# Recurrence layer: casts of summed weights and copies out of PSUM laid out as waiting tasks

## The chip, the cores and the metric

The kernel runs as one program on one core of a Trainium2 chip. The metric is the device time of one execution in microseconds (us). The engines of the core are TensorE (PE: matmuls, with weight loads PEld beside them), VectorE (DVE), ScalarE (ACT), GpSimd (POOL) and SyncE (SP), which here issues most DMA transfers. Each engine runs its instructions in the order of the program and waits on semaphores for the others.

## The reference

A decoder trunk of two layers on one sequence of 1024 rows and 1024 columns. The first layer mixes tokens with a gated linear recurrence of 8 heads of 128 columns, the second with attention in a window; each is followed by a gated feed-forward part with a convolution. Only the first mixer is touched:

```python
q, f, i, g = jnp.split(h @ w_in, 4, axis=-1)
fg = lb + (1.0 - lb) * jax.nn.sigmoid(heads(f))
o = hgrn2_chunkwise(jax.nn.silu(heads(q)), 1.0 - fg, heads(i), jnp.log(fg))
o = o * lax.rsqrt(jnp.mean(jnp.square(o), -1, keepdims=True) + RMS_EPS)
o = o * g_norm_w * jax.nn.silu(heads(g))
return o.reshape(B, S, D) @ w_out
# hgrn2_chunkwise: S_t = diag(f_t) S_{t-1} + k_t v_t^T ; o_t = S_t^T q_t
```

All values are float32.

## The kernel before, in words

The recurrence layer fills the span from about 45 to 535 us. Matmuls of float32 operands are made of three passes (lines 194, 195, 196): high part by high part, high by low, low by high. A high part is a cast on ACT, the low part is a subtraction on DVE (line 169).

**Units and products.** Head 0 is projected directly. The other heads come as units, two per head: `q` (columns of q and f) and `v` (columns of i and g), numbered 0 to 13. A unit is a product of 2x2 blocks made with seven block products instead of eight, p = 1 to 7, which need sums of blocks of the weights and of the input. Each product has 12 matmuls of 128x512 in one of four PSUM banks (`psmm`, buffers 489 to 492). The units run in the order p = 1, 5, 4 (of the unit before), 6, 2, 3, 7.

**Weights.** `unit_load` loads a unit's raw weights by SP into a pair of buffers (raw0 and raw1 for `q`, raw2 and raw3 for `v`; raw_99 to raw_102 in the order's rows). `prepare` makes the weights of the next unit's products while a unit runs: `cast` puts the high part into the tile `WR` on ACT (L1243), and a job makes the low part on DVE (L169). The products 5, 6, 7 and 4 need a sum of blocks first, made in place on DVE (L1250, and L1449 for unit 0).

**Recurrence of a head.** `recur(h)` runs for head h between the products: DVE builds up products of decay over levels (qp, kp and tot, L1089 to L1094), PE makes the scores (`psax` from L200), DVE picks them by masks into `Ab` (L1032, L1053), ACT copies them into `A`, PE transposes kp and the values VT (L204) and multiplies. `turn_values` transposes VT for the next head's use and applies the gate of g. `norm` scales by the mean square, with a power on POOL, and transposes og.

**Out of PSUM.** `collect` takes each product out of its bank: ACT copies the first (L1298 for p=1, L1308 for p=6, L1310 for p=5 or 7, L1349 for VT's second half), DVE adds the second to it (L1342, L1315, L1322).

**What sets the order.** The code is run once on the host with a model of time in the class `Order`: `od.t` is the modelled time of PE, `od.v` that of DVE. A task is a generator that yields the time it waits; `tick`, called between matmuls, steps the tasks whose time has come and lays waiting DVE jobs (`lay_job`) while DVE's modelled queue is short. `need` lays jobs until a certain one is out. `drive` steps all tasks until a condition holds. What comes out is a fixed order of instructions for each engine; the times in the model are not measured.

Of the kernel before, what the change touches and what calls it, by code (L numbers as in the profile page):

```python
# [16 lines left out]
P = 128  # L17
# [90 lines left out]
def trunk(ctx: ExitStack, tc: tile.TileContext, a: dict, out: bass.AP):  # L108
# [591 lines left out]
    with tc.tile_pool(name="t", bufs=1, reuse_waits="tile") as raws, hgrn_pool as hp:  # L700
# [529 lines left out]
        units = [(kind, h) for h in range(1, NH) for kind in "qv"]  # L1230
        raw_of, guard, ready, gated, turned = {}, [[] for _ in range(4)], [], {0}, set()
# [5 lines left out]
        def unit_load(u):  # L1237
            kind, h = units[u]
            raw_of[u] = [halves(column(g, h)) for g in ((0, 1) if kind == "q" else (2, 3))]
# [6 lines left out]
        def prepare(u, stage):  # L1246
            if u >= len(units):
                return
            (b11, b21), (b12, b22) = [(r[:, 0], r[:, 1]) for r in raw_of[u]]
# [10 lines left out]
            else:  # L1260
                after, src = {5: (1, b11), 6: (2, b22), 7: (3, b12), 4: (4, b21)}[stage]
                need(("sum", u, after))
                cast(u, stage, src)

        def product(u, p):
            need(("lo", u, p))
            ps, w = bank(u, p), WR[0][:, row_of(u, p), :]
            od.finish(guard[banks.index(ps)])
            guard[banks.index(ps)] = []
# [10 lines left out]
        state, sigs, turning = {}, [], []  # L1280
# [4 lines left out]

        def collect(u, p, ps):
            kind, h = units[u]
            n = banks.index(ps)
            if p == 1:
                state[u] = {"n": 0}  # L1290
                if kind == "q":
                    if u:
                        drive(lambda: gates_read[0] >= h - 1)
                    state[u]["q"] = hp.tile([P, S], F32, name="qs" if u else "og")
                else:
                    drive(lambda: all(t[1] is None for t in sigs) and queries_done[0] >= 0)
                    sigs.clear()
                nc.scalar.copy((state[u]["q"] if kind == "q" else VT)[:, :512], ps)  # L1298
                return
            st = state[u]  # L1300
            if p in (5, 6, 7) and "c" not in st:
                if kind == "q":
                    drive(lambda: (queries_done if h > 1 else gates_read)[0] >= h - 1)
                else:
                    drive(lambda: h < 2 or h - 2 in turned)
                st["c"] = hp.tile([P, S], F32, name="fg") if kind == "q" else flat(gates[h % 2])
            if p == 6:
                nc.scalar.copy(st["c"][:, :512], ps)  # L1308
            elif p in (5, 7) and "half" not in st:
# [656 lines left out]
```

## Time and profile before

| what | us |
|---|---|
| median of 3 runs | 2181.5 (2179.52 to 2184.3) |
| the profiled execution, its own time | 2183.3 |
| its span in the profile | 2181.5 |
| PE busy in the span | 2112.6 |

The granted clock of PE in the profiled execution was 0.983 on the mean. A line of a view names the engine, the line of the kernel's file, the operation, what it writes and reads (out<-in), and the shape. In brackets stands how long the engine was idle before it and what ended the idle time. psmm and psax are PSUM banks; T and HL hold the input's parts and sums, WR the weights' parts.

### The profile page before, as it was taken

What the parts mean: (1) busy time and instruction counts of PE and PEld (TensorE: products, weight loads), DVE (VectorE), ACT (ScalarE), POOL (GpSimd) and SP (SyncE); (2) the same over time, 40 slices, a digit from 0 to 9 for tenths busy, and PEclk for the clock granted to TensorE, in tenths of its full rate; (3) what the DMA queues carried; (4) which work ended last, traced back from release to release, by engine and by line L of the source; (5) the groups of instructions that cost most, each with busy time, mean ns of one, the idle gap of its engine ahead of it and who ended that gap; (6) DMA issues with size and microseconds to landing.
All of it is one profiled execution on the core that took longest, in us unless ns stands there. A gap on an engine that the chain in (4) does not pass through costs nothing.

```text
span 2181.5 us, 31770 instructions
## 1 busy us (share of the span) xinstructions
PE 2112.6 (97%) x12303; PEld 1758.8 (81%) x12303; DVE 1800.1 (83%) x2459; ACT 973.5 (45%) x1570; POOL 254.2 (12%) x278
## 2 busy tenths in 40 slices
PE   9789999998899999999999999999999999999998
PEld 7667777787688888888888888888888888888887
DVE  6677777765899999997897858978999999978986
ACT  6454445562344444444443256752454444444430
POOL 1000000000103112110000203231021122100001
PEclk9899999999999999999999999999999999999999
DMA  4011111132324547754965431133245577549662
GB/s 158 20 39 42 49 49 49 51 100 95 118 97 153 176 154 168 164 131 147 325 226 183 159 79 34 45 100 114 91 136 179 164 160 167 137 136 321 233 207 102
DMA packets 241488, 286.82 MB, mean 131 GB/s; under 512 B 30089, under 2 KB 160313, under 8 KB 241337
## 3 DMA queue, kind: packets, MB, share of 16 engines
q1 hardware_dynamic: 222464, 238.26, 33.6%
q0 software_dynamic: 18016, 46.16, 10.2%
q8 instruction: 97, 1.59, 0.3%
q14 instruction: 55, 0.44, 0.1%
q10 hardware_dynamic: 856, 0.37, 0.1%
HBM read 241.72 MB, written 89.15 MB: 152 GB/s over the span
## 4 chain that ended last, share of the span: by engine, by line
PE 92%; DVE 5%; ACT 1%; DMA 1%; issue 0%; SPq 0%; DVEq 0%; ACTq 0%
PE psmm L194 18%; PE psmm L196 18%; PE psmm L195 18%; PE psax L194 9%; PE psax L195 9%; PE psax L196 9%; PE psax L200 4%; PE psmm L204 1%; PE psmm L200 1%; PE psax L204 1%; PE psax L1740 1%; DVE WR L169 1%; DVE qp L1089 1%; DVE Ab L1032 1%; PE psmm L1574 1%; DVE kp L1091 1%
## 5 line engine op out<-in xcount | busy, mean ns | idle before, releaser
L498 DVE SCALAR_TENSOR_TENSOR Y<-Y,cwt 128x1023 f32<-128x1023 f32 (+1 forms) x176 | 224.9, 1281 | 48.8 <-ACT Y L496 47.5
L221 ACT CAST HL<-rx 128x1024 fp32r<-128x1024 f32 (+1 forms) x151 | 150.8, 1006 | 147.6 <-DMA rx<-in_ffn_w_in_dram 28.8
L194 PE MATMUL psmm<-T,HL 128*128 128x512 f32 x512 | 200.7, 392 | 0.0
L196 PE MATMUL psmm<-T,HL 128*128 128x512 f32 x512 | 199.4, 389 | 0.0
L195 PE MATMUL psmm<-T,HL 128*128 128x512 f32 x512 | 199.3, 389 | 0.0
L169 DVE TENSOR_TENSOR HL<-rx,HL 128x1024 fp32r<-128x1024 f32 (+1 forms) x151 | 178.4, 1187 | 15.0 <-ACT HL L221 14.8
L496 ACT ACTIVATE Y<-Y,cwt 128x1024 f32<-128x1024 f32 x88 | 108.7, 1238 | 91.5 <-DVE Y L485 86.3
L194 PE MATMUL psax<-T,HL 128*128 128x512 f32 x352 | 137.3, 390 | 0.0
L196 PE MATMUL psax<-T,HL 128*128 128x512 f32 x352 | 137.0, 389 | 0.0
L195 PE MATMUL psax<-T,HL 128*128 128x512 f32 x352 | 137.0, 389 | 0.0
L243 POOL TENSOR_TENSOR rs<-rs,nhalf 128x1 f32<-128x1 f32 x32 | 44.4, 1388 | 738.1 <-DVE rs L242 738.1
L196 PEld LDWEIGHTS psmm<-T,HL 128*128 128x128 f32 x512 | 96.1, 188 | 20.2
L194 PEld LDWEIGHTS psmm<-T,HL 128*128 128x128 f32 x512 | 96.2, 188 | 19.6
L195 PEld LDWEIGHTS psmm<-T,HL 128*128 128x128 f32 x512 | 96.2, 188 | 19.4
L540 POOL COPY warm<-Y 128x1 f32<-128x1 f32 x64 | 64.6, 1009 | 355.4 <-DVE Y L479 350.7
L221 ACT CAST HT<-rx 128x1024 fp32r<-128x1024 f32 (+1 forms) x37 | 35.5, 959 | 133.8 <-DVE rx L452 59.0
L196 PE MATMUL psmm<-T,WR 128*128 128x512 f32 x224 | 89.7, 401 | 5.6 <-DVE WR L169 5.6
L194 PE MATMUL psmm<-T,WR 128*128 128x512 f32 x224 | 91.5, 409 | 2.7 <-ACT WR L1243 2.7
L169 DVE TENSOR_TENSOR WR<-raw,WR 128x512 fp32r<-128x512 f32 x98 | 63.8, 686 | 30.6 <-ACT WR L1243 30.6
L195 PE MATMUL psmm<-T,WR 128*128 128x512 f32 x224 | 88.7, 396 | 0.0
L221 ACT CAST HL<-Y 128x1024 fp32r<-128x1024 f32 (+1 forms) x32 | 28.6, 892 | 117.8 <-DVE Y L452 41.5
L1243 ACT CAST WR<-raw 128x512 fp32r<-128x512 f32 x98 | 58.5, 621 | 48.3 <-DVE raw L1250 30.6
(414 smaller groups left out, 6011.9 us busy)
## 6 DMA issues: line engine op xcount, KB each, us to landing
rx<-in_ffn_w_in_dram SPq DMA_DIRECT2D x136, 256.0 KB, 4.1
rx<-gd SPq DMA_DIRECT2D x118, 256.0 KB, 3.4
bsd<-in_ffn_w_out_dram POOLq DMA_DIRECT2D x36, 768.0 KB, 7.3
gd<-Y SPq DMA_DIRECT2D x44, 512.0 KB, 2.9
raw<-in_hgrn_w_in_dram SPq DMA_DIRECT2D x30, 512.0 KB, 4.1
rx<-in_ffn_w_out_dram SPq DMA_DIRECT2D x54, 256.0 KB, 4.7
R<-bsd SPq DMA_DIRECT2D x44, 256.0 KB, 5.0
Y<-in_ffn_w_in_dram SPq DMA_DIRECT2D x40, 256.0 KB, 4.0
```

Source lines behind the costliest of these rows:

```text
L169: make = lambda e: e.tensor_tensor(lo, src, hi.bitcast(F32), op=ALU.subtract)
L194: nc.tensor.matmul(ps, st(0), mv(0), start=start, stop=False, skip_group_check=more)
L195: nc.tensor.matmul(ps, st(0), mv(1), start=False, stop=False, skip_group_check=more)
L196: nc.tensor.matmul(ps, st(1), mv(0), start=False, stop=stop, skip_group_check=more)
L200: nc.tensor.matmul(ps, lhsT, rhs, start=start, stop=stop, **kw)
L204: nc.tensor.transpose(ps, src, ident)
L221: nc.scalar.copy(hi, src)
L243: nc.gpsimd.tensor_tensor(rs, rs, nhalf, op=ALU.pow)
L496: nc.scalar.activation(c, u, AF.Identity, bias=cwt[:, l, 3, ci:ci + 1], scale=cwt[:, l, 2, ci:ci + 1])
L498: nc.vector.scalar_tensor_tensor(c[:, sh:], u[:, :S - sh], cwt[:, l, 2 - sh, ci:ci + 1], c[:, sh:], op0=ALU.mult, op1=ALU.add)
L540: with tc.issue_after(nc.gpsimd.tensor_copy(tick, Y[:, 2 * (fc % 2) + (p == 4), :1]).ins):
L1243: nc.scalar.copy(w[:, :512], src)
```

## The change

The work is the same on every engine, instruction for instruction; only its order changes. Four things are done.

- The casts of summed weights (products 5, 6, 7, 4) become tasks, `cast_sum`, that wait until the sum has been laid out and until DVE's modelled time has been reached by PE's. A product drives the tasks until its cast is out.
- The copies out of PSUM become tasks (`keep_first`, `keep`, `add_to`, `sum11`), which are laid out when their own conditions hold, instead of driving all others until they do. `clear` waits for a bank's tasks. `drive` now steps the earliest task and moves the modelled time on.
- The raw loads of a later unit and of the output weights become tasks that wait for the low part of p=4.
- The sums of the input are made in another order (those for p=5 ahead of those for p=3), and `first_unit` no longer has all sums of unit 0's weights laid out ahead of the first head's recurrence.

The diff, cut to its core:

```diff
...
             return ROW[p] if p in ROW else (6 if u % 2 else 7)
 
         def unit_load(u):
+            while u > 1 and ("lo", u - 2, 4) not in done_jobs:
+                yield 0.2
             kind, h = units[u]
             raw_of[u] = [halves(column(g, h)) for g in ((0, 1) if kind == "q" else (2, 3))]
 
...
         def prepare(u, stage):
             if u >= len(units):
                 return
+            drive(lambda: u in raw_of)
             (b11, b21), (b12, b22) = [(r[:, 0], r[:, 1]) for r in raw_of[u]]
             plus = lambda key, x, y: job(0.0, 0.61, lambda: tt(x, x, y, op=add), ("sum", u, key))
             if stage == 0:
...
                 cast(u, 2, b21)
                 plus(4, b21, b22)
             else:
-                after, src = {5: (1, b11), 6: (2, b22), 7: (3, b12), 4: (4, b21)}[stage]
-                need(("sum", u, after))
-                cast(u, stage, src)
+                prep[u, stage] = od.spawn(cast_sum(u, stage, *{5: (1, b11), 6: (2, b22), 7: (3, b12), 4: (4, b21)}[stage]))
+
+        def cast_sum(u, p, after, src):
+            while ("sum", u, after) not in done_jobs:
+                yield 0.2
+            yield max(od.v - od.t, 0.0)
+            cast(u, p, src)
 
         def product(u, p):
+            if (u, p) in prep:
+                drive(lambda: prep[u, p][1] is None)
             need(("lo", u, p))
             ps, w = bank(u, p), WR[0][:, row_of(u, p), :]
-            od.finish(guard[banks.index(ps)])
-            guard[banks.index(ps)] = []
+            clear(banks.index(ps))
             moving = {1: lambda j, k: T[:, j, k, :512], 2: lambda j, k: T[:, j, 4 + k, :512],
                       4: lambda j, k: T[:, j, 4 + k, 512:], 5: lambda j, k: T[:, j, k, 512:],
                       6: lambda j, k: tx(0)[:, j, k, :], 7: lambda j, k: tx(1)[:, j, k, :],
...
                 od.tick()
             collect(u, p, ps)
 
-        state, sigs, turning = {}, [], []
+        state, turning, prep = {}, [], {}
 
         def later(n, delay, make):
             task = od.later(delay, make)
             guard[n].append(task)
+
+        def clear(n):
+            drive(lambda: all(t[1] is None for t in guard[n]))
+            guard[n] = []
+
+        def once(n, gen):
+            task = od.spawn(gen)
+            od.step(task)
+            guard[n].append(task)
+
+        def keep_first(u, ps):
+            kind, h = units[u]
+            st = state[u]
+            if kind == "q":
+                while u and gates_read[0] < h - 1:
+                    yield 0.2
+                st["q"] = hp.tile([P, S], F32, name="qs" if u else "og")
+            else:
+                while queries_done[0] < 0 or "asked" not in state[u - 1]:
+                    yield 0.2
+            nc.scalar.copy((st["q"] if kind == "q" else VT)[:, :512], ps)
+            st["kept"] = True
+
+        def keep(u, ps, cols):
+            kind, h = units[u]
+            st = state[u]
+            if kind == "q":
+                while (queries_done if h > 1 else gates_read)[0] < h - 1:
+                    yield 0.2
+            else:
+                while h > 1 and h - 2 not in turned:
+                    yield 0.2
+            if "c" not in st:
+                st["c"] = hp.tile([P, S], F32, name="fg") if kind == "q" else flat(gates[h % 2])
+            nc.scalar.copy(st["c"][:, cols], ps)
+            st[cols.start] = True
+
+        def add_to(u, ps, cols, i):
+            st = state[u]
+            while cols.start not in st:
+                yield 0.2
+            yield 0.2
+            tt(st["c"][:, cols], st["c"][:, cols], ps, op=add)
+            od.vec(0.61)
+            od.spawn(second(u, i), 0.8)
 
         def collect(u, p, ps):
             kind, h = units[u]
             n = banks.index(ps)
             if p == 1:
-                state[u] = {"n": 0}
-                if kind == "q":
-                    if u:
-                        drive(lambda: gates_read[0] >= h - 1)
-                    state[u]["q"] = hp.tile([P, S], F32, name="qs" if u else "og")
-                else:
-                    drive(lambda: all(t[1] is None for t in sigs) and queries_done[0] >= 0)
-                    sigs.clear()
-                nc.scalar.copy((state[u]["q"] if kind == "q" else VT)[:, :512], ps)
+                state[u] = {"n": 0, "left": [5, 7]}
+                once(n, keep_first(u, ps))
                 return
             st = state[u]
-            if p in (5, 6, 7) and "c" not in st:
-                if kind == "q":
-                    drive(lambda: (queries_done if h > 1 else gates_read)[0] >= h - 1)
-                else:
-                    drive(lambda: h < 2 or h - 2 in turned)
-                st["c"] = hp.tile([P, S], F32, name="fg") if kind == "q" else flat(gates[h % 2])
             if p == 6:
-                nc.scalar.copy(st["c"][:, :512], ps)
-            elif p in (5, 7) and "half" not in st:
-                nc.scalar.copy(st["c"][:, 512:], ps)
-                st["half"] = True
+                once(n, keep(u, ps, slice(0, 512)))
             elif p in (5, 7):
-
-                def sum22():
-                    tt(st["c"][:, 512:], st["c"][:, 512:], ps, op=add)
-                    od.vec(0.61)
-                    od.spawn(second(u, 1), 0.8)
-                later(n, 0.2, sum22)
+                st["left"].remove(p)
+                cols = slice(512, 1024)
+                once(n, keep(u, ps, cols) if st["left"] else add_to(u, ps, cols, 1))
             elif p == 3:
-
-                def sum12():
-                    tt(st["c"][:, :512], st["c"][:, :512], banks[3], op=add)
-                    od.vec(0.61)
-                    od.spawn(second(u, 0), 0.8)
-                later(3, 0.2, sum12)
+                once(n, add_to(u, ps, slice(0, 512), 0))
             elif p in (2, 4):
                 first(u, 0 if p == 2 else 1, ps, n)
 
...
             kind, h = units[u]
             st, ts = state[u], slice(i * 512, (i + 1) * 512)
             if i == 0:
-                dst = (st["q"] if kind == "q" else VT)[:, ts]
 
                 def sum11():
+                    while "kept" not in st:
+                        yield 0.2
+                    yield 0.2
+                    dst = (st["q"] if kind == "q" else VT)[:, ts]
                     tt(dst, dst, ps, op=add)
                     od.vec(0.61)
                     if kind == "q":
-                        sigs.append(od.spawn(first_query(u), 0.8))
-                later(n, 0.2, sum11)
+                        od.spawn(first_query(u), 0.8)
+                once(n, sum11())
                 return
             if kind == "v":
                 nc.scalar.copy(VT[:, ts], ps)
...
             yield 0.8
             tt(q, q, sig, op=ALU.mult)
             od.vec(0.61)
+            state[u]["asked"] = True
             made(u)
 
         def second(u, i):
...
             turning.clear()
 
         def drive(cond):
-            n = 0
-            while not cond():
-                for t in sorted(od.chains, key=lambda k: k[0]):
-                    if t is not params:
-                        od.step(t)
-                    if cond():
-                        return
-                if jobs:
+            for n in range(9999):
+                if cond():
+                    return
+                task = min((t for t in od.chains if t is not params), key=lambda t: t[0])
+                od.t = max(od.t, task[0])
+                od.step(task)
+                while jobs and od.v < od.t + 1.5:
                     lay_job()
-                od.t = max(od.t, od.v)
-                n += 1
-                if n > 999:
-                    raise ValueError("the order never comes to its end")
+            raise ValueError("the order never comes to its end")
 
         def build_sums(go):
             for t in range(4):
...
                 for which in (7, 6):
                     split_sum(t, which)
                     yield 1.0
-            for t in range(4):
-                split_sum(t, 3)
-                yield 1.0
-            while not go:
-                yield 0.2
-            for t in range(4):
-                split_sum(t, 5)
-                yield 1.0
+            left = {5: [0, 1, 2, 3], 3: [0, 1, 2, 3]}
+            while left[5] or left[3]:
+                which = 5 if left[5] and (go or not left[3]) else 3
+                while which == 5 and not go:
+                    yield 0.2
+                split_sum(left[which].pop(0), which)
+                yield 0.8
 
         prepared, WR, ring_pool = [], [], ExitStack()
 
         def first_unit():
-            while ("x", 5, 3) not in done_jobs:
+            while ("x", 5, 3) not in done_jobs or ("x", 3, 3) not in done_jobs:
                 yield 0.2
             staging.close()
             pool = ring_pool.enter_context(tc.tile_pool(name="wr", bufs=1, reuse_waits="tile"))
...
             cast(0, 1, b11)
             cast(0, 2, b21)
             plus(1, b11, b12)
-            yield 1.6
-            need(("sum", 0, 1))
-            cast(0, 5, b11)
+            prepare(0, 5)
+            yield 1.2
             cast(0, 3, b22)
             plus(3, b12, b22)
             plus(2, b22, b11)
-            yield 1.6
             for stage in (6, 7):
                 prepare(0, stage)
-                yield 1.6
             plus(4, b21, b22)
             prepare(0, 4)
             prepared.append(0)
...
         rows1 = lambda k: [(0, P, wo[k * P:(k + 1) * P, :])]
         out_us, oraw = [], []
 
+        def out_load():
+            while ("lo", last, 4) not in done_jobs:
+                yield 0.2
+            for k in range(4):
+                oraw.append(load4(out_loads(rows1, 0, (2 * k, 2 * k + 1))))
+
         def out_split(u):
+            drive(lambda: u < len(oraw))
             hl = hl_at(u)
             nc.scalar.copy(hl[:, 0], oraw[u])
             job(1.2, 1.22, lambda: low_part(hl[:, 1], oraw[u], hl[:, 0], None), ("out", u))
...
                         if p in stages:
                             prepare(v + 1, stages[p])
                         if p == 6 and u + 2 <= last:
-                            need(("lo", u, 4))
-                            unit_load(u + 2)
+                            od.spawn(unit_load(u + 2))
                         if v == last - 1 and p == 4:
-                            need(("lo", last, 4))
-                            for k in range(4):
-                                oraw.append(load4(out_loads(rows1, 0, (2 * k, 2 * k + 1))))
+                            od.spawn(out_load())
                     else:
                         r = ROW.get(p, 6)
                         if r < 6:

...
```

In what follows the rows are those of one engine's program: line, operation, out<-in, shape.

DVE at the start, in unit 0 and head 0; raw_99 and raw_100 are the unit's weights, St, qp, kp and kd belong to `recur(0)`. Before:

```order
L1449 TENSOR_TENSOR raw_100<-raw_100 128x512
L1449 TENSOR_TENSOR raw_100<-raw_100,raw_99 128x512
L169 TENSOR_TENSOR WR<-raw_100,WR 128x512 x2
L1449 TENSOR_TENSOR raw_99<-raw_99,raw_100 128x512
L169 TENSOR_TENSOR WR<-raw_99,WR 128x512
L1100 TENSOR_TENSOR St<-qs,kp 128x1024
L1101 TENSOR_TENSOR qp<-qs,fg 128x1024
```

After:

```order
L1109 TENSOR_TENSOR kd<-kp,qp 128x512 x2
L1375 TENSOR_TENSOR og<-og,psmm 128x512
L1399 TENSOR_TENSOR og<-og,GT 128x512
L1089 TENSOR_TENSOR qp<-qp,tot 128x256x2
L1091 TENSOR_TENSOR kp<-kp,tot 128x256x2
L1094 TENSOR_TENSOR tot<-tot 128x256
L1478 TENSOR_TENSOR raw_99<-raw_99,raw_100 128x512
L169 TENSOR_TENSOR WR<-raw_100,WR 128x512
L1478 TENSOR_TENSOR raw_100<-raw_100 128x512
```

The sums of unit 0's weights (L1449 before, L1478 now), the first of which p=5 needs, stood ahead of the head's chain and now stand behind its first part.

ACT in the head whose VT copy stands at 207.54 us in the profile; raw_101 and raw_102 hold the next unit's weights. Before:

```order
L1076 COPY kd<-qp 128x32x16
L1077 COPY kd<-kp 128x32x16
L1310 COPY fg<-psmm 128x512
L1243 CAST WR<-raw_101 128x512
L1349 COPY VT<-psmm 128x512
L1243 CAST WR<-raw_99 128x512
L1396 COPY VG<-psax 128x1024
```

After (a line with dots stands for rows left out):

```order
L1076 COPY kd<-qp 128x32x16
L1077 COPY kd<-kp 128x32x16
L1328 COPY fg<-psmm 128x512
L1382 COPY VT<-psmm 128x512
L1430 COPY VG<-psax 128x1024
...
L1246 CAST WR<-raw_99 128x512
L1436 ACTIVATE VT<-VG 128x1024
L1328 COPY fg<-psmm 128x512
...
L1397 ACTIVATE VT<-qs 128x512
L1246 CAST WR<-raw_101 128x512
L1246 CAST WR<-raw_102 128x512
```

The cast of the summed weight from raw_101 (p=5) stood between the copies of fg and VT; it now stands behind the sigmoid of q (L1397), and the cast from raw_99 (p=4) behind the copy of VG.

DVE in the same head; raw_100 here is the weight of p=6. Before:

```order
L169 TENSOR_TENSOR WR<-raw_100,WR 128x512
L1089 TENSOR_TENSOR qp<-qp,tot 128x128x4
L1091 TENSOR_TENSOR kp<-kp,tot 128x128x4
L1094 TENSOR_TENSOR tot<-tot 128x128
L169 TENSOR_TENSOR WR<-raw_99,WR 128x512
```

After:

```order
L1053 COPY_PREDICATED Ab<-msk,psax 128x32x4
L1089 TENSOR_TENSOR qp<-qp,tot 128x32x16
L1091 TENSOR_TENSOR kp<-kp,tot 128x32x16
L1094 TENSOR_TENSOR tot<-tot 128x32
L1053 COPY_PREDICATED Ab<-msk,psax 128x16x8
L1032 COPY_PREDICATED Ab<-msk,psax 128x64x2 x2
L169 TENSOR_TENSOR WR<-raw_100,WR 128x512
L1089 TENSOR_TENSOR qp<-qp,tot 128x16x32
```

The low part of p=6 stood ahead of the third level of the chain (128x128x4); it now stands behind the fifth (128x32x16) and behind the picking into Ab.

More of the change, by code (lines that the diff above doesn't have):

```diff
@@ L1230, in trunk @@
         units = [(kind, h) for h in range(1, NH) for kind in "qv"]
+        last = len(units) - 1
         raw_of, guard, ready, gated, turned = {}, [[] for _ in range(4)], [], {0}, set()
@@ L1494, in trunk @@
             firsts = [od.spawn(build_sums(go))]
-            unit_load(0)
+            list(unit_load(0))
             qs = hp.tile([P, S], F32, name="qs")
@@ L1516, in trunk @@
                     firsts.append(od.spawn(first_unit()))
-                    unit_load(1)
+                    list(unit_load(1))
             ready.append((0, (qs, fg, kp)))
@@ L1535, in trunk @@
             od.tick()
-            last = len(units) - 1
             stages = {1: 0, 5: 5, 6: 6, 7: 7, 2: 2, 4: 4}
```

## The prediction

> **What bounds the kernel now.** I read the page first: its busy shares and the chain of work that ended last.
>
> ```profile
> span 2181.5 us, 31770 instructions
> PE 2112.6 (97%) x12303; PEld 1758.8 (81%) x12303; DVE 1800.1 (83%) x2459; ACT 973.5 (45%) x1570; POOL 254.2 (12%) x278
> PE 92%; DVE 5%; ACT 1%; DMA 1%; issue 0%; SPq 0%; DVEq 0%; ACTq 0%
> ```
>
> TensorE (PE) is the bound, 92% of the chain. The change neither adds nor removes work on it, so only its idle time, and time at a reduced clock, can be won. The next view is the list of PE's waits, limited to the first 560 us, which hold the recurrence; its columns are the waiting group, what it waited for, total, count, longest.
>
> ```profile
> PE psax L204 <- ACT VT L1349: 21.3, 6, 3.9
> ...
> PE psmm L194 <- DVE Y L351: 4.3, 1, 4.3
> ...
> PE psmm L1574 <- DVE HL L169: 2.4, 1, 2.4
> ```
>
> The first row is the largest: the transposes of VT wait for a copy out of PSUM, six times. The timeline of one such place (start, duration, engine, line, operation, idle before and its releaser) tells why:
>
> ```profile
> 199.49 0.50 PE L194 MATMUL psmm<-T,WR 128*128 128x512 f32 x1
> 199.61 0.69 DVE L1089 TENSOR_TENSOR qp<-qp,tot 128x512 f32<-128x512 f32 x1 [2.42 <-PE psax L200]
> 201.46 0.58 ACT L1310 COPY fg<-psmm 128x512 f32<-128x512 f32 x1
> 204.48 1.91 DVE L169 TENSOR_TENSOR WR<-raw,WR 128x512 fp32r<-128x512 f32 x3
> 206.30 0.69 DVE L1250 TENSOR_TENSOR raw<-raw,raw 128x512 f32<-128x512 f32 x1
> 207.02 0.62 ACT L1243 CAST WR<-raw 128x512 fp32r<-128x512 f32 x1 [4.98 <-DVE raw L1250]
> 207.54 0.58 ACT L1349 COPY VT<-psmm 128x512 f32<-128x512 f32 x1
> 208.18 1.11 PE L204 MATMUL psax<-ident,VT 128*128 128x128 f32 x4 [3.85 <-ACT VT L1349]
> ```
>
> The rows are in order of time, from three engines. The VT copy itself takes 0.58 us and its operand lies in PSUM in time. It stands in ScalarE's (ACT's) queue behind the cast of a summed weight (L1243), which idles 4.98 us for the sum at 206.30, which stands in VectorE's (DVE's) queue behind three low parts, and these behind the recurrence's chain (199.61 to 204.5). The same 3.85 stands at 208.18, 265.27, 322.82, 379.03 and 435.54; the sixth is the first head's, 2.07.
>
> A stall costs more than its idle time. The table of stretches (us, busy time and count, granted PE clock, DMA share, GB/s) gives the clock right behind the five, and behind the sixth and the 2.4:
>
> ```profile
> 208.18:213.20 5.02, 5.02 (x105) 0.50 0.01 3
> 265.27:271.22 5.95, 5.95 (x107) 0.50 0.01 4
> 322.42:325.84 3.42, 3.02 (x101) 0.50 0.00 0
> 379.03:383.86 4.83, 4.83 (x107) 0.65 0.02 5
> 435.54:441.89 6.35, 6.00 (x108) 0.50 0.01 3
> 153.00:156.40 3.40, 3.22 (x106) 1.00 0.02 5
> 496.50:499.92 3.42, 3.17 (x7) 0.50 0.00 0
> ```
>
> Clock lost on busy time is 2.51 + 2.98 + 1.51 + 1.69 + 3.00 = 11.7 us, 2.3 per stall. After an idle stretch of 2.07 us nothing was lost; one of 2.44 us (the row of L1574) was followed by half clock. The limit lies between, or depends on where a stretch falls.
>
> **The heads.** The change moves those casts behind the VT copy, so the five stalls go: 5 x 3.85 = 19.3 us idle and 11.7 of clock, 31.0 together. What is late next? The low parts move too. In every other head (that of 208 us is one) the low part of the weights of p=6 now stands behind the whole chain. That chain ends at 204.48, where the first of the three low parts starts now; one low part is a third of the 1.91, some 0.7, so it is ready at 205.2. PE has at 199.49 three matmuls of p=5, twelve of p=4 and the first two of p=6 before it needs that half. Matmuls follow each other every 0.227 us:
>
> ```profile
> 213.54 0.39 PE L194 MATMUL psmm<-T,WR 128*128 128x512 f32 x1
> 213.77 0.39 PE L195 MATMUL psmm<-T,WR 128*128 128x512 f32 x1
> ```
>
> 17 x 0.227 = 3.9, so PE arrives at 203.4 and waits 1.8. In the other heads it is the low part of p=7, moved behind the product of q and its sigmoid:
>
> ```profile
> 276.28 1.09 PE L204 MATMUL psax<-ident,kp 128*128 128x128 f32 x8
> 278.37 0.63 ACT L1364 ACTIVATE VT<-qs 128x512 f32<-128x512 f32 x1
> 279.04 0.69 DVE L1366 TENSOR_TENSOR qs<-qs,VT 128x512 f32<-128x512 f32 x1 [2.35 <-ACT VT L1364]
> ```
>
> The product ends at 279.7, a low part behind it at 280.3. PE ends the transposes at about 277.3 and has six matmuls of p=3 and two of p=7, 1.8 us, so it is there at 279.1 and waits 1.2. Three heads of the first kind and two of the second: 3 x 1.8 + 2 x 1.2 = 7.8 us, all under 2.07, so I charge them no clock. Lower bound of their price: 0, if the chain runs a little earlier; upper: 7.8 and 11.7 of clock as behind the old stalls. The heads give 31.0 - 7.8 = 23.2.
>
> [...]
>
> **The start.** Up to p=6 of unit 3 (some 180 us) the two orders hold the same PE work, and the stalls that change are these:
>
> ```profile
> 82.77 0.50 PE L194 MATMUL psmm<-HL,WR 128*128 128x512 f32 x1 [4.02 <-ACT fg L1310]
> 101.42 0.79 PE L196 MATMUL psmm<-T,WR 128*128 128x512 f32 x1 [5.59 <-DVE WR L169]
> 141.18 1.97 PE L204 MATMUL psax<-ident,og 128*128 128x128 f32 x8 [6.92 <-DVE og L1204]
> 153.18 0.65 PE L204 MATMUL psax<-ident,VT 128*128 128x128 f32 x4 [2.07 <-ACT VT L1349]
> ```
>
> and the clock behind the first three of them (the stretch's us, then busy time and count of PE, its weight loads, DVE, ACT and POOL, granted clock, DMA share, GB/s):
>
> ```profile
> 82.77:86.90 4.13, 4.13 (x11) 3.29 (x12) 2.52 (x5) 1.72 (x3) 0.00 (x0) 0.59 0.00 0
> 101.42:107.38 5.96, 5.96 (x14) 4.70 (x15) 2.95 (x5) 1.10 (x2) 0.00 (x0) 0.50 0.01 3
> 141.18:144.93 3.75, 3.75 (x32) 2.70 (x36) 2.56 (x5) 1.11 (x1) 0.00 (x0) 0.50 0.01 4
> ```
>
> All four go: 4.02 + 5.59 + 6.92 + 2.07 = 18.6 idle, and 1.7 + 3.0 + 1.9 = 6.6 of clock, 25.2. In their place DVE does the first head's chain before the sums of unit 0:
>
> ```profile
> 65.69 1.29 DVE L169 TENSOR_TENSOR WR<-raw,WR 128x512 fp32r<-128x512 f32 x2 [0.73 <-ACT WR L1243]
> 74.77 1.22 DVE L1100 TENSOR_TENSOR St<-qs,kp 128x1024 f32<-128x1024 f32 x1
> 79.70 1.28 DVE L1109 TENSOR_TENSOR kd<-kp,qp 128x512 f32<-128x512 f32 x2
> ```
>
> From 74.77 to the end of 79.70 that chain takes 6.2 us; og's sum and product and one more level, five rows of about 0.6, follow it. Starting at 67.0 it ends near 76; with the sum (0.6) and the cast (0.6) and the hops between the engines the weights of p=5 come at about 78.3, where PE, done with two products at 73.3, has idled 5.0. Their low part stands some fourteen rows of 0.6 further on, at 86.75: PE, after two matmuls, idles 8.05 more. By the same counting p=6 waits 2.6 for its high and 3.1 for its low part, and a VT transpose 0.55: 19.3 idle. I charge clock three times at the mean of the three old ones, 2.2: 6.6. The start thus loses 25.9 - 25.2 = 0.7. Bounds: 4 better, if the last two cost no clock; 5 worse, if one more does, and DVE's rows slip by half a chain.
>
> **The rest** I cost at nothing. The raw loads of a unit are issued later on SP, behind the low part of p=4, which moves by half a unit at most:
>
> ```profile
> raw<-in_hgrn_w_in_dram SPq DMA_DIRECT2D x30, 512.0 KB, 4.1
> 216.65 23.44 SPq L721 DMA_DIRECT2D raw<-in_hgrn_w_in_dram  x4
> ```
>
> (the page's list of DMA issues, with the us to landing, and SP's timeline) a pair of loads is issued at 216.7, the next unit's some 23 us later, and two pairs of buffers take turns, so that a pair is wanted about a unit (28 us) after its issue; 14 us later and 4.1 to land leave 10. The stores of yd, which change places with them, are read only at the layer's end. The loads of the output weights now stand behind four loads of WR; their cover is the last head's scores, and if it fails the 2.4 of L1574 comes again, no more than it costs now. The layer's end moves with PE: the loads of Y are issued as PE ends its pass.
>
> ```profile
> 530.84 0.39 PE L196 MATMUL psax<-HL,T 128*128 128x512 f32 x1
> 531.11 4.03 SPq L330 DMA_DIRECT2D Y<-in_x_dram  x8
> ```
>
> The sum: 23.2 - 0.7 = 22.5 us. The profiled execution took 2183.3 (1.8 outside its span), 1.8 above the median of three runs, 2181.5: 2160.8 on its own scale, 2159 against the median. What a measurement of this kernel can tell from no change is about 0.2%, 4.4 us.
>
> **The rivals.**
>
> Dearer waits: the new stalls of 1.2 to 1.8 are each followed by half clock, as the 2.44 was. Against it stands the 2.07 without. 11.7 us are lost again: 2171.
>
> Cheaper waits: the chain on DVE runs ahead, no low part is late, and the start is at its better bound: 7.8 + 4.7 more: 2147. For it speaks that DVE idles 2.42 us before 199.61; against it, that this idle time waits for PE itself.
>
> Slower: DVE becomes the limit of every head. If the fused multiply of the gate or the gate's own product, 1.2 to 1.3 us each (the same number of elements as L1100), slides between the chain and the low part, and that with its releasers late, the new wait grows one for one. With its clock it costs s + 2.3 in each head against 6.2 now, so from s = 3.8 on, allowing for the start, nothing is won; at s = 4.7 five heads cost 35.0 against 31.0 and the start 0.7: 2186. Against it: those rows stand where DVE now waits for PE.
>
> No change: the next stage's loads end when they do now, and the 4.3 us at Y grows by what is won: 2181.5. Against it, the row of 531.11 above.
>
> **How the numbers follow.** The forecast 0.50, dearer waits 0.22, cheaper waits 0.18, no change 0.04, slower 0.06. Faster is the sum of the first three, 0.90. The range of 2147 to 2174 reaches from the cheaper case to the dearer one with the start 3 worse, and leaves out the last two and the tails.
>
> **What would show it.** Right: no PE wait of 3.85 for VT; in its place waits of 1 to 2 us for WR's low part (L169) at p=6 and p=7 in turn; PE's stalls of 5 and 8 us near 73 and 79 for WR; none for og near 141; a head's period of about 52.5 us where 57 stood. Wrong: waits for WR over 2.4 with half clock behind them in every head, more than 26 us lost before 180 us, or a wait for HL above 5 us near the end of the layer.

## The result and the profile after

The changed kernel takes 2169.8 us (median of four runs, 2169.2 to 2170.9), against 2180.5 before (four runs; the 2181.5 of the prediction is the median of the first three): a ratio of 0.995, with a 95% interval of 0.9933 to 0.9967. That is 10.7 us faster, where I had forecast 22.5 and a range of 2147 to 2174.

The page after, its span and the busy time of the engines:

```profile
span 2167.7 us, 31744 instructions
PE 2103.1 (97%) x12303; PEld 1751.8 (81%) x12303; DVE 1800.9 (83%) x2459; ACT 971.8 (45%) x1570; POOL 254.4 (12%) x278
```

PE runs the same 12303 matmuls and is busy 9.5 us less: time at half clock counts as busy (from 208.54 to 211.95 after, at a granted clock of 0.50, 3.41 of 3.41 us are busy), so a part of the gain is clock. PE's waits in the first 560 us:

```profile
PE psmm L196 <- DVE WR L169: 24.3, 7, 7.3
PE psmm L194 <- ACT WR L1246: 11.5, 3, 6.2
PE psax L204 <- ACT VT L1382: 5.5, 2, 3.3
PE psmm L195 <- DVE TX L169: 2.3, 1, 2.3
...
PE psmm L194 <- DVE Y L351: 0.3, 1, 0.3
```

The 21.3 us for the VT copy have become 5.5; in their place PE waits 24.3 us for low parts of WR (L169), where it was 5.6 before, and 11.5 for high parts (L1246), where it was 2.7. The seven waits of the first row, and the three of the second, lie here (PE's timeline, only its rows with idle time):

```profile
66.11 0.50 PE L194 MATMUL psmm<-T,WR 128*128 128x512 f32 x1 [2.70 <-ACT WR L1246]
78.35 0.79 PE L194 MATMUL psmm<-T,WR 128*128 128x512 f32 x1 [6.23 <-ACT WR L1246]
86.83 0.79 PE L196 MATMUL psmm<-T,WR 128*128 128x512 f32 x1 [7.26 <-DVE WR L169]
96.86 0.51 PE L194 MATMUL psmm<-HL,WR 128*128 128x512 f32 x1 [2.57 <-ACT WR L1246]
100.54 0.79 PE L196 MATMUL psmm<-HL,WR 128*128 128x512 f32 x1 [2.95 <-DVE WR L169]
154.35 0.66 PE L204 MATMUL psax<-ident,VT 128*128 128x128 f32 x4 [2.28 <-ACT VT L1382]
207.57 0.50 PE L196 MATMUL psmm<-HL,WR 128*128 128x512 f32 x1 [3.43 <-DVE WR L169]
273.91 0.50 PE L196 MATMUL psmm<-HL,WR 128*128 128x512 f32 x1 [1.17 <-DVE WR L169]
316.07 0.50 PE L196 MATMUL psmm<-HL,WR 128*128 128x512 f32 x1 [3.48 <-DVE WR L169]
380.95 0.50 PE L196 MATMUL psmm<-HL,WR 128*128 128x512 f32 x1 [1.17 <-DVE WR L169]
424.44 0.80 PE L196 MATMUL psmm<-HL,WR 128*128 128x512 f32 x1 [4.84 <-DVE WR L169]
477.59 0.66 PE L204 MATMUL psax<-ident,VT 128*128 128x128 f32 x4 [3.25 <-ACT VT L1382]
```

The places are those of the prediction: long waits for p=5 (78.35, 86.83) and p=6 (96.86, 100.54) in the start, then p=6 and p=7 in turn. But the wait at p=6 is 3.4 to 4.8, not 1.8.

Where the time came from can be read by counting. Both kernels have 1176 matmuls on WR in the same order of products. The start of the n-th, after less before, tells what has been won up to there:

| n-th matmul on WR | before, us | after, us | difference |
|---|---|---|---|
| 0 | 65.7 | 66.1 | +0.4 |
| 336 (unit 4) | 194.4 | 195.5 | +1.2 |
| 504 (unit 6) | 251.5 | 251.6 | +0.2 |
| 672 (unit 8) | 309.0 | 304.0 | -5.0 |
| 840 (unit 10) | 365.2 | 358.6 | -6.6 |
| 1008 (unit 12) | 421.7 | 411.0 | -10.7 |
| 1050 (unit 12) | 443.3 | 433.1 | -10.2 |
| 1134 (unit 13) | 470.2 | 461.0 | -9.2 |

The start loses 0.8. The heads with the wait at p=7 win 5.2 and 4.1 us. Those with the wait at p=6 win 1.0 and 1.6 and the last of them gives 1.5 back (up to the 1134th). At the layer's end the wait for Y (L351) shrinks from 4.3 to 0.3 us, and with it the difference is 10.7 at that place. That this equals the difference of the medians is chance: the two profiled executions end 13.8 us apart, since the half clock behind the 4.3 (534.0 to 540.9 before, at 0.50; from 520 to 530 after it is 1.00) goes too, and the one before, 2183.3, is itself 2.8 above its median.

Why the wait at p=6 is twice what I worked out stands on the queues of SP, ACT and DVE at the first of these places, after the change, in order of time:

```profile
197.71 0.99 SPq L721 DMA_DIRECT2D raw<-in_hgrn_w_in_dram  x2
200.09 0.69 DVE L1089 TENSOR_TENSOR qp<-qp,tot 128x512 f32<-128x512 f32 x1 [1.11 <-PE psax L200]
201.73 0.62 ACT L1246 CAST WR<-raw 128x512 fp32r<-128x512 f32 x1 [5.41 <-DMA raw<-in_hgrn_w_in_dram]
203.28 0.62 ACT L1246 CAST WR<-raw 128x512 fp32r<-128x512 f32 x1 [0.92 <-DMA raw<-in_hgrn_w_in_dram]
203.81 0.61 ACT L1076 COPY kd<-qp 128x512 f32<-128x512 f32 x1
204.45 0.69 DVE L1089 TENSOR_TENSOR qp<-qp,tot 128x512 f32<-128x512 f32 x1 [1.76 <-ACT kd L1076]
206.80 0.71 DVE L169 TENSOR_TENSOR WR<-raw,WR 128x512 fp32r<-128x512 f32 x1
```

The raw loads of a later unit are issued at 197.7. ACT's next two instructions are the casts for p=1 and p=3 of that unit: it idles 5.41 and 0.92 us for the loads. The recurrence's copies into kd stand behind the casts, though qp was ready at 200.8; DVE's next level waits 1.76 us for them, and the low part of p=6, which stands behind that chain, starts at 206.80. In the kernel before, the same loads and the same two casts lie far apart:

```profile
182.09 0.99 SPq L721 DMA_DIRECT2D raw<-in_hgrn_w_in_dram  x2
195.03 1.14 ACT L1243 CAST WR<-raw 128x512 fp32r<-128x512 f32 x2
```

They are 12.9 us apart, not the 28 that I had assumed, and the change moved the load by 15.6 (1.2 of it because the whole kernel is late by that much at this place). ACT's waits for such loads between 180 and 460 us, none of which stands in that list before:

```profile
ACT WR L1246 <- DMA raw<-in_hgrn_w_in_dram: 28.7, 10, 5.6
```

In the last such head the delay is greater: between the casts and the copies stand four transfers of conv weights that ACT itself issues (from 418.90 to 420.63), DVE idles 3.17 us for kd, and the wait is the 4.84 at 424.44.

### The profile page after: what moved, and what is told of

It is laid out like the page before. It is cut to its first block, busy times and chain, and to the rows that moved or that the text cites. A ratio compares the mean times of both kernels' runs of the same rounds, so it can differ in the third digit from the quotient of the medians.

```text
span 2167.7 us, 31744 instructions
## 1 busy us (share of the span) xinstructions
PE 2103.1 (97%) x12303; PEld 1751.8 (81%) x12303; DVE 1800.9 (83%) x2459; ACT 971.8 (45%) x1570; POOL 254.4 (12%) x278
## 3 DMA queue, kind: packets, MB, share of 16 engines
q0 software_dynamic: 18016, 46.16, 10.2%
## 4 chain that ended last, share of the span: by engine, by line
PE 87%; DVE 6%; ACT 3%; DMA 3%; issue 1%; SPq 0%; ACTq 0%; DVEq 0%
PE psmm L196 17%; PE psmm L194 17%; PE psmm L195 17%; PE psax L194 9%; PE psax L195 9%; PE psax L196 9%; PE psax L200 3%; PE psmm L204 1%; PE psmm L200 1%; DMA raw<-in_hgrn_w_in_dram 1%; PE psax L1769 1%; PE psax L204 1%; DVE qp L1089 1%; PE psmm L1603 1%; DVE WR L169 1%
## 5 line engine op out<-in xcount | busy, mean ns | idle before, releaser
L169 DVE TENSOR_TENSOR HL<-rx,HL 128x1024 fp32r<-128x1024 f32 (+1 forms) x151 | 178.6, 1189 | 17.9 <-ACT HL L221 17.7
L540 POOL COPY warm<-Y 128x1 f32<-128x1 f32 x64 | 64.5, 1008 | 356.0 <-DVE Y L479 351.2
L169 DVE TENSOR_TENSOR WR<-raw,WR 128x512 fp32r<-128x512 f32 x98 | 65.3, 688 | 24.2 <-ACT WR L1246 24.2
L196 PE MATMUL psmm<-HL,WR 128*128 128x512 f32 x168 | 68.6, 409 | 17.1 <-DVE WR L169 17.1
L1246 ACT CAST WR<-raw 128x512 fp32r<-128x512 f32 x98 | 58.7, 618 | 52.7 <-DMA raw<-in_hgrn_w_in_dram 34.8
```

Of the source, the lines that this page charges most:

```text
L169: make = lambda e: e.tensor_tensor(lo, src, hi.bitcast(F32), op=ALU.subtract)
L196: nc.tensor.matmul(ps, st(1), mv(0), start=False, stop=stop, skip_group_check=more)
L540: with tc.issue_after(nc.gpsimd.tensor_copy(tick, Y[:, 2 * (fc % 2) + (p == 4), :1]).ins):
L1246: nc.scalar.copy(w[:, :512], src)
```

## The experiments

The theory after the result: the heads' gain went to the raw loads that the change moved; the casts that wait for them hold up ACT, and with it the chain that the low part of p=6 now stands behind. The rival: that low part's place alone makes the wait. All times are medians; each kernel was compared with the kernel before on its own chip, whose medians there were 2179.6 to 2181.6, so that differences of 2 or 3 us between two experiments on different chips say little.

**e1_raw_early.** The loads where they were:

```diff
+            elif stage == 4 and u:
+                need(("sum", u, 4))
+                cast(u, 4, b21)
             else:
                 prep[u, stage] = od.spawn(cast_sum(
...
-                            od.spawn(unit_load(u + 2))
+                            drive(lambda: (u, 4) not in prep or prep[u, 4][1] is None)
+                            need(("lo", u, 4))
+                            list(unit_load(u + 2))
```

> The changed kernel, with the cast for p=4 made at once again, so that its low part comes early and a later unit's raw loads are issued on SP where they were before the change; all else as changed. Theory (late loads): in the changed kernel ScalarE stands 5.4 us at a cast that waits for the raw load, the recurrence's copies into kd stand behind that cast, VectorE idles 1.8 to 3.2 us for them, and so the low part of p=6 is late. Then the waits for raw loads go from ScalarE, the three stalls of 3.4, 3.5 and 4.8 us at p=6 fall to 1.5 to 1.9, as I had forecast, and with them half clock behind two of them: 5 + 4 to 5 us, so 2158 to 2163. Rival (the low part's place): the chain on VectorE is what makes p=6 wait, the load only fills time that is idle anyway: stalls stay near 3.4 and the time within 2 us of the changed kernel's 2170.

It took 2156.0 us, 0.9884 of before (0.9869 to 0.9899), 13.8 less than the changed kernel. PE's waits between 180 and 460 us are these:

```profile
PE psmm L194 <- ACT fg L1331: 2.0, 1, 2.0
PE psax L204 <- ACT VT L1385: 1.2, 2, 0.9
```

No wait for WR is left at all, and the time lies below the 2158 to 2163 of the theory, so more went than I expected: the edit also brought the low part of p=6 ahead of the chain again, as its program shows. It tells that the loads or the place matter, not which. The next two kernels separate them.

**e6_late_cast.** Loads as late as in the changed kernel, the low part of p=6 still behind the chain; only the two casts stand further back on ACT:

```diff
             if stage == 0:
-                cast(u, 1, b11)
-                cast(u, 3, b22)
...
+                def head():
+                    yield max(landed[u] - od.t, 0.0)
+                    cast(u, 1, b11)
+                    cast(u, 3, b22)
...
+                prep[u, 1] = prep[u, 3] = od.spawn(head())
...
```

with landed[u] set to the modelled time of the load's issue plus 5. The unit's first three sums go back with the two casts.

> The changed kernel with the loads as late as the change made them, but with the two casts that wait for them (p=1 and p=3) a few rows further back on ScalarE, behind the copies into kd; the low part of p=6 stays behind the chain. Theory (the casts that wait for a load hold up the copies into kd): VectorE's idle time of 1.8, 1.8 and 3.2 us for those copies goes, the stalls at p=6 of 3.4, 3.5 and 4.8 us fall to about 1.7, and half clock behind them goes: 5 us and up to 5 of clock, 2160 to 2165. Rival (the low part's place makes the whole stall): the stalls stay above 3 us and the time within 2 us of 2170.

2156.3 us, 0.9885 (0.987 to 0.99). ACT and DVE at the place shown above, and PE's wait there:

```profile
200.11 0.62 ACT L1076 COPY kd<-qp 128x512 f32<-128x512 f32 x1 [4.49 <-DVE qp L1089]
201.91 0.68 DVE L1089 TENSOR_TENSOR qp<-qp,tot 128x512 f32<-128x512 f32 x1
202.56 0.62 ACT L1247 CAST WR<-raw 128x512 fp32r<-128x512 f32 x1 [0.70 <-DMA raw<-in_hgrn_w_in_dram]
204.25 0.71 DVE L169 TENSOR_TENSOR WR<-raw,WR 128x512 fp32r<-128x512 f32 x1
205.01 0.50 PE L196 MATMUL psmm<-HL,WR 128*128 128x512 f32 x1 [1.56 <-DVE WR L169]
```

```profile
PE psmm L196 <- DVE WR L169: 4.7, 3, 1.6
```

The copies into kd go first, DVE's chain runs on without a gap, and the three waits at p=6 are 1.56 each, close to the 1.8 of the prediction. The casts wait 0.7 instead of 5.4. Up to the 1050th matmul on WR this kernel wins 23.6 us in the heads (from +0.5 to -23.1), against 11.4 in the changed kernel and 23.2 in my sum. Of the 12.2 us between the two kernels, 11.1 lie in the three heads with the wait at p=6. So it is the casts waiting for the loads that took the missing half. That the 1.17 at p=7 went too was not expected; the order there is another: the low part of p=7, which ran at 273.17 in the changed kernel, behind the product of q and its sigmoid, runs at 259.06 here.

**e7_p6_now.** Loads and casts late, but the cast for p=6 made at once, so that its low part stands ahead of the chain:

```diff
+            elif stage == 6 and u:
+                need(("sum", u, 2))
+                cast(u, 6, b22)
```

> The changed kernel with the casts for p=6 made at once again (not for unit 0), so that the low part of p=6 stands ahead of the chain; loads as late as in the changed kernel. Theory (place and load add up): the stalls at p=6 go, but VectorE still idles some 1.8 us for the copies into kd in every other head, and PE waits that much at the next scores or transposes: a third to a half of what the early loads won (13.8 us), 2162 to 2166. Rival (the place is all): no stall comes instead, and it is as fast as the kernel with the early loads, 2155 to 2159.

2157.9 us, 0.9892 (0.9877 to 0.9907): my theory's number was missed, the rival's is right. Two rows of it between 180 and 460 us, ACT's longest wait for loads and PE's first:

```profile
ACT WR L1246 <- DMA raw<-in_hgrn_w_in_dram: 27.6, 10, 5.5
PE psax L204 <- ACT VT L1385: 2.8, 3, 1.7
```

ACT waits for loads as long as before, and almost none of it reaches PE. So the wait of 3.4 needed both: a late load on ACT and a low part that stands behind the chain on DVE. Taking away either is enough for the wait at p=6.

**e9_casts_now.** All casts of summed weights made at once, as in the kernel before; copies out of PSUM as tasks and the new start:

```diff
+            elif u:
+                key, src = {5: (1, b11), 6: (2, b22), 7: (3, b12), 4: (4, b21)}[stage]
+                need(("sum", u, key))
+                cast(u, stage, src)
             else:
...
```

(for u > 0; unit 0 keeps the tasks).

> The changed kernel with all casts of summed weights made at once again, each forcing its sum to be laid out first (not for unit 0); copies out of PSUM and loads as tasks, new start. Theory (without waiting casts the sums and low parts are forced ahead of the recurrence's chain on VectorE, or a cast stands before the VT copy): stalls of 2 to 4 us come in every head, at the scores or at VT; 2163 to 2174. Rival (the copies as tasks and the new start carry the whole gain, and the casts as tasks only bring the late loads): no such stall, 2154 to 2159, as with the early loads.

2154.2 us, 0.9877 (0.9861 to 0.9893), the fastest of all, 15.6 below the changed kernel. Here too the rival is right. In this kernel the cast of p=5 stands ahead of the VT copy again, as before the change, yet its sum is forced out ahead of the chain's later levels on DVE:

```profile
197.34 0.68 DVE L1254 TENSOR_TENSOR raw<-raw,raw 128x512 f32<-128x512 f32 x1
198.80 0.69 DVE L1089 TENSOR_TENSOR qp<-qp,tot 128x512 f32<-128x512 f32 x1 [0.78 <-PE psax L200]
```

No wait of 3.85 comes: what made PE wait was the sum behind the chain, not the cast ahead of the copy. The waiting casts, a part that the change is named after, cost more than they brought. By the experiments their price is that of the late loads: here the loads are early again, and ACT has no wait for them left in the heads; e6, which keeps the waiting casts and the late loads and only takes the hold on ACT away, is within 2.1 us of this kernel.

**e4_casts_only.** The other way round: the kernel before with the waiting casts for p=5, 6 and 7 alone. In one unit the cast of p=7 comes after its raw buffers are loaded anew, so that those weights are others than the reference's; the work on every engine is the same.

```diff
-                need(("sum", u, after))
-                cast(u, stage, src)
+                if stage == 4 or not u:
+                    need(("sum", u, after))
+                    cast(u, stage, src)
+                else:
+                    prep[u, stage] = od.spawn(cast_sum(u, stage, after, src))
...
```

> The kernel before, with one part of the change alone: the casts of the summed weights for p=5, 6 and 7 are waiting tasks (not p=4, not unit 0); copies out of PSUM, loads, start and end as before. Theory (the casts ahead of the VT copy made the five stalls of 3.85 us): those go, waits of 1 to 2 us at p=6 and p=7 come in their place, the raw loads stay early, so more is won than with the whole change: 18 to 24 us, 2157 to 2163. Rival (the copies must be tasks as well): with the driving copies kept, the order model falls back into laying casts first, and the 3.85 stay: 2178 to 2182.

2190.4 us, 1.0042 (1.0028 to 1.0056): slower, which neither expected. PE's waits between 180 and 460 us:

```profile
PE psmm L196 <- DVE WR L169: 14.7, 6, 3.4
PE psax L1000 <- ACT A L1070: 0.2, 1, 0.2
```

The VT waits are gone, as the theory had it, and 12.0 us are won from the 336th to the 1050th matmul. But up to the 336th 14.3 are lost. The next two kernels say what that goes with: e3, which has waiting casts and the old start too, loses 14.7 up to there, while e11, with the old start and casts at once, wins 4.6.

**e3_old_start and e11_now_old_start.** The changed kernel, and e9_casts_now, with all of unit 0's sums and casts ahead of head 0's recurrence:

```diff
-            prepare(0, 5)
-            yield 1.2
+            yield 1.6
+            need(("sum", 0, 1))
+            cast(0, 5, b11)
...
-            for stage in (6, 7):
-                prepare(0, stage)
+            for key, p, src in ((2, 6, b22), (3, 7, b12)):
+                need(("sum", 0, key))
+                cast(0, p, src)
+                yield 1.6
...
```

> The changed kernel with unit 0's sums and casts laid out ahead of the first head's recurrence again, as before the change. Theory (the start is nearly a draw, 0.8 us lost by the trace at the 210th matmul on WR): the stalls of 6.2, 7.3, 2.6 and 3.0 us before 105 us go and others of about the same sum come: 2167 to 2171. Rival (the new start is dear, since half clock stands there for 24 us): the old one is 4 us or more faster, 2166 or less.

> The kernel whose casts of summed weights are all made at once (2154.2), with the old start: all of unit 0's sums and casts ahead of the first head's recurrence. It completes the square of casts (waiting, at once) and start (new, old). Theory (the new start is worth some 11 us by itself, as with waiting casts): 2162 to 2168. Rival (the old start was only bad together with waiting casts, whose tasks pile up behind it): within 3 us of the new start, 2151 to 2158; then the copies out of PSUM as tasks carry the whole gain.

| | new start | old start |
|---|---|---|
| waiting casts | 2169.8 (the change) | 2181.3 (e3, ratio 1.0003, 0.9993 to 1.0013) |
| casts at once | 2154.2 (e9) | 2160.0 (e11, ratio 0.9903, 0.9889 to 0.9918) |

The theory for e3 is refuted, and its rival too. By the traces the changed kernel's start draws with that of the kernel before, but against the old start among the change's other parts it wins 11.5 us; with casts at once, 5.8, between the two numbers expected of e11. PE's longest waits from 60 to 235 us in e3 (in an execution of 2186.0, the longest of its ten):

```profile
PE psmm L196 <- DVE WR L169: 14.1, 4, 6.0
PE psmm L194 <- ACT WR L1246: 10.7, 3, 5.0
PE psmm L194 <- ACT fg L1328: 9.7, 2, 5.1
```

Waits for WR of both kinds are there, as in the changed kernel (13.6 and 11.5 in that stretch), and 9.7 for the fg copy besides. What is left of the gain in e11, 20 us, cannot be the casts nor the start, so by elimination it is the copies out of PSUM as tasks, with the new `drive`, the loads as tasks and the order of the input's sums; these were not parted, so that this is argued and not shown.

**e8_early_p5 and e10_now_p5.** The kernel e1, and e9, with p=5 of unit 0 ahead of the recurrence:

```diff
-            prepare(0, 5)
+            need(("sum", 0, 1))
+            cast(0, 5, b11)
+            need(("lo", 0, 5))
```

> The kernel with the early loads (2156), and in unit 0 the sum, the cast and the low part for p=5 ahead of the first head's recurrence, the rest of unit 0 behind it. Theory (the stalls of 5.0 and 7.3 us before 90 us come from p=5's sum and low part standing behind the recurrence's chain): both go, the chain starts some 2.5 us later, waits of a few us come for p=6: 4 to 9 us are won, 2147 to 2152. Rival (the chain's start is what matters there, as in the old start): what is won at p=5 is lost behind, 2154 to 2158.

> The kernel whose casts of summed weights are all made at once (2154.2), and in unit 0 the sum, the cast and the low part for p=5 ahead of the first head's recurrence. Theory (the stalls of 5.0 and 7.3 us at p=5 of unit 0 are that sum's and low part's; with the other casts made at once nothing behind gives it back): 4 to 9 us faster, 2145 to 2150. Rival (as in the kernel with early loads and p=5 first, where 9.7 us were won up to the 252nd matmul on WR and 9.9 lost up to the 294th, at casts that stood behind the longer chain of head 0): the same loss, 2153 to 2160.

2159.5 (0.9899, 0.9882 to 0.9916) and 2157.5 (0.9898, 0.988 to 0.9916): nothing won, for either base. PE's longest waits from 60 to 235 us in e10:

```profile
PE psmm L194 <- ACT WR L1246: 9.8, 2, 7.1
PE psax L204 <- ACT VT L1386: 3.8, 1, 3.8
PE psax L200 <- ACT kd L1158: 3.2, 1, 3.2
```

The wait for p=5 is gone and one of 7.1 for p=6 stands in its place; two more, of 3.2 and 3.8, come later. The start's idle time is moved about, not removed.

**e5_tail_early.** The changed kernel with the loads of the output weights ahead of those into WR:

```diff
-                            od.spawn(out_load())
+                            drive(lambda: (last, 4) not in prep or prep[last, 4][1] is None)
+                            need(("lo", last, 4))
+                            list(out_load())
```

> The changed kernel with the loads of the output weights issued where they were before the change, ahead of the loads into WR. Theory (the last head's stall of 3.25 us at the transposes of VT comes from ScalarE, which stood 3.6 us at a cast of output weights that waited for its load): that wait goes, the stall falls below 1 us, and half clock behind it goes: 3 to 5 us, 2165 to 2167. Rival (the end of the layer is set elsewhere, by the loads of Y or by the low parts of the output weights, as the 2.4 us stall before): the stall moves there and the time stays, 2169 to 2171.

2171.6 us, 0.9954 (0.9939 to 0.9969): the rival, 0.6 above its range. PE's waits from 460 to 530 us:

```profile
PE psmm L194 <- DVE Y L351: 3.6, 1, 3.6
PE psmm L1605 <- DVE HL L169: 1.8, 1, 1.8
```

The 3.25 at VT is gone, and the wait for Y is back at 3.6, that for HL at 1.8. The time stays.

## Why the prediction was right or wrong

*What bounds, and the five stalls.* Right. The 3.85 for VT went in all five heads, and waits for the low part came at p=6 and p=7 in turn. A head took 52.4 us where the wait is at p=7, and 56.1 and 54.7 where it is at p=6; 52.5 was forecast for both.

*The waits at p=7.* Forecast 1.2; measured 1.17 and 1.17.

*The waits at p=6.* Forecast 1.8; measured 3.43, 3.48 and 4.84, and 1.56 in e6. The counting of rows on DVE and PE was right. What was missing is the 1.76 (3.17 in the last) that DVE waits for ACT inside the chain.

*The step that failed* is the one that costed the raw loads at nothing because 10 us of cover were left. I took a unit's length, 28 us, for the time from issue to first use; the row of SP and the row of ACT in the trace of before put it at 12.9, the load takes 4.1 by the page, and the shift was 15.6 where I allowed 14. Without the 1.2 by which all is late there, the shift is 14.4, so it was sized well; the cover was not. 14.4 and 4.1 are 5.6 more than 12.9, and ACT idles 5.41. The instruction that waits for the load has others queued behind it, a path that the prediction does not have. It halves the heads' term: 23.2 forecast, 11.4 measured, and 23.6 with the two casts out of the way. The waits at p=6 show it too: 11.75 us idle and 4.7 of clock (the rows below) where 5.4 stood in the sum.

*Clock.* I charged none for the new heads' waits. Behind the two of 1.17 there was none (1.00 from 273.91 to 277.30 and from 380.95 to 384.40), and behind the 1.56 at 414.14 in e6 the next matmuls followed each other every 0.23 us, as with no wait. Behind the longer ones:

```profile
207.57:212.00 4.43, 4.43 (x102) 0.61 0.00 0
316.07:319.50 3.43, 3.43 (x109) 1.00 0.00 0
423.58:430.41 6.83, 5.97 (x110) 0.50 0.01 2
```

So the rival of dearer waits (2171) has nearly the number that was measured, but by luck and not by its mechanism: the waits of its size were followed by no loss of clock; two of the three longer ones were, at 0.61 and 0.50.

*The start.* Forecast 0.7 lost, measured 0.8 (+0.4 to +1.2). Term by term: 6.2, 7.3, 2.6, 3.0 and 2.3 for VT, where I had 5.0, 8.05, 2.6, 3.1 and 0.55. That is 2.0 us more idle time than forecast, at about the clock that I charged (6.2 for 6.6). That the total still fits is partly luck: behind the wait of 2.7 at 66 us, which both kernels have and which I left out of the sum, the kernel before runs 3.41 us at half clock (66.42 to 69.83), 1.7 us lost, and the changed one does not.

*The rest.* The output weights' load came late as feared: 3.25 at VT in the last head in place of the 2.4 for HL. That this costs no more than before held by the sum, since the wait for Y fell by 4.0.

*The range and the chances.* The time lies in the range; the likeliest case had half its size. One slip in the cheaper case changes nothing: the start is counted there as 4.7 better, where its bound is 4, and the time is 2147 with either.

## What to carry to other kernels

Before a load is costed at nothing, read its issue and its first reader from the trace as two rows, and compare the gap with the shift. Look too at what its engine runs behind that reader: here it was not the cast's own consumer that was late, but the copies behind it, which wait for no load (qp was ready at 200.8, the first copy started at 203.81). And when one change bundles several moves, undo each by itself: here making the casts of summed weights wait, with the late loads that this brought, cost 15.6 us of what the others had won.

## What the runs showed of the hardware

Two idle stretches of nearly the same length were followed by different clocks: after 3.43 us (207.57) PE ran at a granted clock of 0.61 on the mean for 4.4 us, after 3.48 us (316.07) at 1.00. After 2.07 and 2.28 us (153.18 before, 154.35 after) the clock stayed at 1.00; after 2.44 (496.75 before) it was 0.50. So in these two traces no single length of an idle stretch separates the two cases. Where the stretches fall differs. From 60 to 600 us the half clock comes 20 times, 13 before and 7 after: nine times for 3.41 us, ten times for 6.83 and once for 17.07 (75.42 to 92.49 after). Pieces of 3.41 us, laid end to end from the points where the changed kernel's clock changes, look like this (us, busy time of PE and count, granted clock, DMA share, GB/s):

```profile
205.13:208.54 3.41, 0.97 (x4) 1.00 0.00 0
208.54:211.95 3.41, 3.41 (x96) 0.50 0.00 0
310.94:314.35 3.41, 1.65 (x8) 1.00 0.06 18
314.35:317.76 3.41, 1.69 (x11) 1.00 0.00 0
```

The 3.43 us lie for the most part in one piece, in which PE is busy for 0.97 us, and the next piece runs at 0.50. The 3.48 us are split over two, with PE busy 1.65 and 1.69 us, and the clock stays at 1.00. The 2.44 us lie in a piece with 1.22 us busy (493.09 to 496.50), followed by 0.50; the 2.28 us leave 1.57 (150.51 to 153.92), followed by 1.00. With both traces cut like this from 60 to 2050 us, the 19 pieces at full clock in which PE idled 1.99 us or more were all followed by half clock. Of those in which it idled less one was, with 1.68 (554.53 before), while the longest idle time with full clock behind it is 1.86 (373.62 before); the ends of matmuls are modelled, so these figures are rough. In these two traces, then, the clock behind a wait goes with PE's idle time in such a piece and not with the length of the wait alone; no run was made to test this by itself.
